# Retention heads with the values projected first, and two of four weight-block sums made by accumulating transfers

## The chip, the core and the metric

The program runs on one core of a Trainium2 chip. TensorE (PE) multiplies, VectorE (DVE) and ScalarE (ACT) do elementwise work and empty PSUM, GpSimd (POOL) does a few small operations, and SyncE (SP) issues the transfers. Each engine works through its own list strictly in order; a semaphore wait in front of an instruction holds up everything behind it on that engine. The metric is the time of one execution on the device, in microseconds; lower is better.

## The reference, cut to what matters

Two layers of a streaming encoder. Each layer projects 528 tokens (16 meta tokens and 512 of the sequence) of width 1024 to 14336 columns, runs a short gated convolution and a retention with four heads on them, gates the two branches and adds them.

```python
for l in range(DEPTH):                                   # DEPTH = 2
    xn = _rmsnorm(h, pre_norm_g[l])
    proj = xn @ w_in[l] + b_in[l]                        # (528, 1024) @ (1024, 14336)
    c_h, c_b, c_c, c_z, r_q, r_k, r_v, r_z, g_a, g_b = jnp.split(proj, split_at, axis=-1)
    y_a = _short_conv_branch(c_h, c_b, c_c, c_z, conv_w[l], conv_b[l], w_conv_out[l])
    y_b = _retention_branch(r_q, r_k, r_v, r_z, ret_gn_g[l], w_ret_out[l])
    y = jax.nn.sigmoid(g_a) * y_a + jax.nn.sigmoid(g_b) * y_b
    h = h + _rmsnorm(y @ w_o[l], post_norm_g[l])

# _retention_branch, one head: dk = 256, dv = 512
q, k = _rope(q, pos), _rope(k, pos) * dk ** -0.5
s = (q @ k.T) * decay_by_distance                        # chunks of 64 tokens
out = s @ v                                              # within a chunk, and over the state
out = (out - mean) * rsqrt(var + GN_EPS) * gn_g * silu(z)
y_b += out @ w_ret_out[rows of this head]
```

## The kernel before

**Products.** Every float32 product is made of three products in PE's float32r format: each operand is split into a high part (a rounded copy, made by ACT, line 142) and a low part (source minus high part, made by DVE, line 143). Activations are kept transposed, feature by token, as two halves of 264 tokens.

**A group.** Most of the input projection is cut into groups of 256 output columns (class `Group`). A group is a two by two block product of Strassen's kind, in Winograd's form, with seven block products instead of eight: `mul` (line 279) issues one of them as 12 matmuls, four slices of the contraction by three float32r passes, so a group is 84 matmuls. On the weight side it needs four sums of blocks: block 0 + block 1 and block 2 + block 1 (line 307, in place, in the upper halves of the staging tiles `raw`), their combination into tile b (line 314), and the fourth, t4 (line 315). Three staging tiles serve a group: a (block 0 and the first sum), b (block 3 and the combination) and c (block 2 and the second sum). SP loads block by block of 256 KB (lines 299, 301, 302). There are six staging tiles, four pairs of split weights (`whi`, `wlo`) and two of the small pair (`whd`, `wld`).

**Order.** The program is a list of jobs written out by hand: groups, output products of a head (`RetOut`, 24 matmuls for each 128 output columns, line 244), output products of the convolution. After each `mul` and after every second contraction slice of an output product `tick()` advances a count, and work put off with `later(delay, fn)` is emitted at the tick it asked for. The last product of a group (`end`) waits in `pending` until the next job has issued its first two; then the group's callback runs: `k_done`, `q_done` (rope, and for q the scores at 8, 10 and 12 ticks), `v_done` (transposing the values, `vtrans`, at 3, 6 and 9 ticks) or `z_done`. `z_done` emits the rest of the head: `attend` (line 481) at 1, 3, 5 and 7 ticks, then the group norm in three steps: `stats` at 10 (line 370, a column sum on PE; line 374 on DVE; line 375, a power, on POOL), `wide` at 13 (line 384, PE spreads the 528 results over the partitions; ACT copies them out, line 387), `finish` at 14 to 17 (DVE scales the four tiles, line 514, and splits them). The next head's output products need all four split tiles. A tile scheduler then fixes the order on each engine; calls in `high_priority` (evictions of PSUM) go ahead of other work.

In the order of a head before, each of heads 1 to 3 projects keys, queries, the first values, then two of the previous head's output products, the second values, the other two, and the two gate groups z. Head 0 of each layer is written out apart and calls the same callbacks.

Of the kernel before, what the change touches and what calls it, by code (L numbers as in the profile page):

```python
# [15 lines left out]
ALU = mybir.AluOpType  # L16
# [40 lines left out]
def trunk(ctx: ExitStack, tc: tile.TileContext, xT, w_in, binT, w_co, w_ro, w_o, gpre, gpost,  # L57
# [19 lines left out]
    def rslot(w=T):  # L77
        return gr.tile([P, w], F32R, tag="r", name=nm("r"))

    def fslot(w=T, dt=F32):  # L80
        return gr.tile([P, w], dt, tag="r", name=nm("f"))
# [45 lines left out]
    def later(delay, fn):  # L127
        now[1] += 1
        heappush(queue, (now[0] + delay, now[1], fn))
# [154 lines left out]
    class Group:  # L284
# [10 lines left out]
        def load(self, j, w):  # L295

            t = self.raw[j] = src()
            if j == 1:
                nc.sync.dma_start(t[:, 512:], w[:, 3, :])
                return  # L300
            nc.sync.dma_start(t[:, 0:512], w[:, j, :])
            nc.sync.dma_start(t[:, 512:], w[:, 1, :])

        def halves(self, j):
            if not j:
                for r in self.raw[0::2]:
                    nc.vector.tensor_tensor(r[:, 512:], r[:, 512:], r[:, 0:512], op=ALU.add)  # L307
            self.w[j] = wtile("whi"), wtile("wlo")
            split(*self.w[j], self.raw[j])

# [79 lines left out]
    def twice(dst, src):  # L390

        nc.scalar.copy(dst.rearrange("p (a b) -> p a b", a=2),
                       src[:, T - CHUNK:T].unsqueeze(1).to_broadcast([P, 2, CHUNK]))
# [402 lines left out]
    for l in range(DEPTH):  # L796
# [20 lines left out]
        def add(job, *args, todo=todo):  # L817
            todo.append((job, args))
            return job

        def k_done(ts, hd):
            a, b, hd["k"] = rope(ts, 0)

            def k8():
                hd["k8"] = rslot(512).rearrange("p (n c) -> p n c", n=4)
                for n in range(4):
                    twice(hd["k8"][:, n, :], hd["k"][n // 2][n % 2].bitcast(F32))
            later(0, a)
            later(2, b)
            later(3, k8)  # L830

        def q_done(ts, hd, h, l, d=8):
            a, b, hd["q"] = rope(ts, QCOLS[l].t0)
            later(0, a)
            later(2, b)

            def tables():
                hd["S"] = [gr.tile([P, SW], F32R, tag="S", name=nm(x), bufs=2) for x in ("Shi", "Slo")]
                nc.sync.dma_start(Dsb, decay[h])
            later(3, tables)  # L840
            for n, js in enumerate(((0,), (1, 2), (3, 4))):
                later(d + 2 * n, lambda js=js: scores(l, hd["q"], hd["k"], hd["k8"], *hd["S"], js))

        def v_done(ts, hd, d=3):
            hd["vt"] = hd.get("vt", []) + list(ts)
            if len(hd["vt"]) == 4:
                vt = hd["vt"]
                v8 = fslot(512).rearrange("p (v c) -> p v c", v=4)
                for v in range(4):
                    twice(v8[:, v, :], vt[v])  # L850
                hd["V"] = V = [(rslot(512), rslot(512)) for _ in JT]
                for n, js in enumerate(((0, 1), (2, 3), (4,))):
                    later(d + 3 * n, lambda js=js: vtrans(vt, v8, V, js))

        def z_done(ts, hd, h, l, yr, silu=(1,)):
            cs = slice(QCOLS[l].t0, T)
            for n in silu:
                nc.scalar.activation(ts[n][:, cs], ts[n][:, cs], AF.Silu)
            hd["zt"] = hd.get("zt", []) + list(ts)
            if len(hd["zt"]) < 4:  # L860
                return

            def start():
                hd["sums"] = fslot()
                hd["n"] = normed(l, hd["zt"], hd["sums"], yr)
            later(0, start)
            for v in range(4):
                later(1 + 2 * v, lambda v=v: attend(l, h, *hd["S"], hd["V"], v, hd["zt"][v], hd["sums"]))
            later(10, lambda: hd["n"][0]())
            later(13, lambda: hd["n"][1]())  # L870
            for v in range(4):
                later(14 + v, lambda v=v: hd["n"][2](v))

        hd["done"] = (k_done, q_done, v_done, z_done)
        yrs = jb["yrs"] = [[] for _ in range(H)]
# [6 lines left out]
        add_conv(0)  # L882
        for h in range(1, H):
            d = {}
            add(Group(l, R_K + h * DK, I_ALL[l], lambda ts, d=d: k_done(ts, d)))
            add(Group(l, R_Q + h * DK, I_Q[l], lambda ts, d=d, h=h, l=l: q_done(ts, d, h, l)))
            add(Group(l, R_V + h * DV, I_ALL[l], lambda ts, d=d: v_done(ts, d)))
            for q in (0, 1):
                add(RetOut(l, h - 1, q), yrs[h - 1])
            add(Group(l, R_V + h * DV + 256, I_ALL[l], lambda ts, d=d: v_done(ts, d)))  # L890
            for q in (2, 3):
                add(RetOut(l, h - 1, q), yrs[h - 1])
            for b in range(2):
                add(Group(l, R_Z + h * DV + b * 256, I_Q[l],
                          lambda ts, d=d, h=h, l=l, yr=yrs[h]: z_done(ts, d, h, l, yr), AF.Silu))
# [364 lines left out]
```

## Time and profile before

| | |
|---|---|
| median of 3 runs | 1603.13 us (1600.23 to 1605.2) |
| profiled execution | 1600.25 us, span of its instructions 1598.4 us |
| PE busy | 1553.9 us, 97% of the span |
| DVE, ACT, POOL busy | 1168.9, 910.2, 28.9 us |
| mean granted TensorE clock | 0.995 |
| transfers | 174.37 MB, mean 109 GB/s |

A matmul's row lasts until its result has left the array, and the next one starts before that; so PE's busy time tells only where it stood still for longer than a matmul's overlap. What a stretch lost is seen from the number of matmuls in it and from the waits of PE. "Idle before" is the time an engine sat still before an instruction, with what released it. PEclk is the granted clock as a share of full speed: 1.00 is 2.4 GHz, 0.5 is 1.2 GHz.

### The profile page before, as it was taken

What the parts mean: (1) busy time and instruction counts of PE and PEld (TensorE: products, weight loads), DVE (VectorE), ACT (ScalarE), POOL (GpSimd) and SP (SyncE); (2) the same over time, 40 slices, a digit from 0 to 9 for tenths busy, and PEclk for the clock granted to TensorE, in tenths of its full rate; (3) what the DMA queues carried; (4) which work ended last, traced back from release to release, by engine and by line L of the source; (5) the groups of instructions that cost most, each with busy time, mean ns of one, the idle gap of its engine ahead of it and who ended that gap; (6) DMA issues with size and microseconds to landing.
All of it is one profiled execution on the core that took longest, in us unless ns stands there. A gap on an engine that the chain in (4) does not pass through costs nothing.

```text
span 1598.4 us, 29227 instructions
## 1 busy us (share of the span) xinstructions
PE 1553.9 (97%) x11762; PEld 1494.1 (93%) x11762; DVE 1168.9 (73%) x1702; ACT 910.2 (57%) x1763; POOL 28.9 (2%) x23
## 2 busy tenths in 40 slices
PE   9999999899999999999999999999999999999998
PEld 9989999898999999999999998998998999999986
DVE  6996966776776788866376889678777777997542
ACT  6675565464565466655345666655654655676531
POOL 0000000001000000000000000000000000000000
PEclk9999999999999999999999999999999999999999
DMA  7132332232222243335321223222322223334421
GB/s 263 67 113 73 106 107 89 83 108 97 89 103 87 91 141 128 133 123 180 119 101 53 100 94 113 103 103 95 111 93 80 101 98 119 132 126 145 142 98 53
DMA packets 86039, 174.37 MB, mean 109 GB/s; under 512 B 11280, under 2 KB 15888, under 8 KB 85904
## 3 DMA queue, kind: packets, MB, share of 16 engines
q1 hardware_dynamic: 85760, 172.50, 31.2%
q8 instruction: 92, 1.51, 0.4%
q14 instruction: 43, 0.35, 0.1%
q10 hardware_dynamic: 144, 0.01, 0.0%
HBM read 168.21 MB, written 4.26 MB: 108 GB/s over the span
## 4 chain that ended last, share of the span: by engine, by line
PE 79%; DVE 10%; ACT 5%; issue 3%; DMA 3%; POOL 1%; SPq 0%; DVEq 0%; POOLq 0%; ACTq 0%
PE pb L279 25%; PE pp L244 15%; PE pc L279 13%; PE pp L648 7%; PE pa L279 6%; PE pp L481 4%; PE pp L1122 3%; PE pb L648 3%; DVE wlo L143 2%; PE pp L422 2%; DMA raw<-in_w_in 2%; ACT whi L142 2%; DVE r L143 1%; PE pp L384 1%; PE pp L447 1%
## 5 line engine op out<-in xcount | busy, mean ns | idle before, releaser
L143 DVE TENSOR_TENSOR wlo<-raw,whi 128x1024 fp32r<-128x1024 f32 (+2 forms) x358 | 392.7, 1107 | 120.4 <-ACT whi L142 117.5
L142 ACT CAST whi<-raw 128x1024 fp32r<-128x1024 f32 (+2 forms) x358 | 339.4, 959 | 227.8 <-PE pp L244 63.7
L279 PE MATMUL pb<-Xh,whi 128*128 128x264 f32 (+2 forms) x1008 | 287.7, 285 | 2.2 <-ACT pa L335 1.2
L279 PE MATMUL pb<-Xl,whi 128*128 128x264 f32 (+2 forms) x1008 | 285.0, 283 | 0.0
L279 PE MATMUL pb<-Xh,wlo 128*128 128x264 f32 (+2 forms) x1008 | 284.7, 283 | 0.1
L244 PE MATMUL pp<-r,whi 128*128 128x264 f32 (+1 forms) x1152 | 251.2, 325 | 5.6 <-ACT r L142 4.8
L279 PE MATMUL pc<-Xh,whi 128*128 128x264 f32 (+2 forms) x672 | 194.4, 289 | 8.1 <-ACT f L325 7.8
L244 PEld LDWEIGHTS pp<-r,whi 128*128 128x128 f32 x1152 | 176.3, 188 | 23.7 <-ACT r L142 5.9
L279 PEld LDWEIGHTS pb<-Xh,whi 128*128 128x128 f32 x1008 | 189.6, 188 | 4.4 <-ACT pa L335 1.6
L279 PE MATMUL pc<-Xl,whi 128*128 128x264 f32 (+2 forms) x672 | 192.0, 286 | 0.0
L279 PE MATMUL pc<-Xh,wlo 128*128 128x264 f32 (+2 forms) x672 | 191.5, 285 | 0.0
L279 PEld LDWEIGHTS pb<-Xl,whi 128*128 128x128 f32 x1008 | 189.6, 188 | 0.6
L279 PEld LDWEIGHTS pb<-Xh,wlo 128*128 128x128 f32 x1008 | 189.3, 188 | 0.5 <-DVE wlo L143 0.3
L244 PE MATMUL pp<-r,wlo 128*128 128x264 f32 (+1 forms) x576 | 153.1, 321 | 1.4 <-DVE wlo L143 1.4
L307 DVE TENSOR_TENSOR raw<-raw 128x512 f32<-128x512 f32 x168 | 115.1, 686 | 41.4 <-DMA raw<-in_w_in 40.9
L279 PEld LDWEIGHTS pc<-Xh,whi 128*128 128x128 f32 x672 | 128.0, 190 | 12.3 <-ACT f L325 11.2
L279 PEld LDWEIGHTS pc<-Xl,whi 128*128 128x128 f32 x672 | 127.9, 190 | 0.4
L279 PEld LDWEIGHTS pc<-Xh,wlo 128*128 128x128 f32 x672 | 127.8, 190 | 0.3
L244 PEld LDWEIGHTS pp<-r,wlo 128*128 128x128 f32 x576 | 95.3, 188 | 9.8 <-DVE wlo L143 2.0
L279 PE MATMUL pb<-Xh,whd 128*128 128x264 f32 (+2 forms) x336 | 96.7, 288 | 1.1 <-ACT f L325 1.1
L279 PE MATMUL pa<-Xh,whi 128*128 128x264 f32 (+2 forms) x336 | 96.7, 288 | 0.0
L279 PE MATMUL pa<-Xl,whi 128*128 128x264 f32 (+2 forms) x336 | 95.7, 285 | 0.0
(219 smaller groups left out, 3300.3 us busy)
## 6 DMA issues: line engine op xcount, KB each, us to landing
raw<-in_w_in SPq DMA_DIRECT2D x426, 256.0 KB, 2.9
raw<-in_w_ro SPq DMA_DIRECT2D x32, 512.0 KB, 3.2
raw<-in_w_in SPq DMA_DIRECT2D x20, 512.0 KB, 4.8
raw<-in_w_co SPq DMA_DIRECT2D x16, 512.0 KB, 3.2
raw<-in_w_o SPq DMA_DIRECT2D x16, 512.0 KB, 3.9
Dsb<-in_decay SPq DMA_DIRECT2D x8, 520.0 KB, 3.9
h1d<-f SPq DMA_DIRECT2D x8, 264.0 KB, 4.5
f<-h1d SPq DMA_DIRECT2D x8, 264.0 KB, 4.3
```

Source lines behind the costliest of these rows:

```text
L142: nc.scalar.copy(dst_hi, src)
L143: nc.vector.tensor_tensor(dst_lo, src, dst_hi.bitcast(F32), op=ALU.subtract)
L244: nc.tensor.matmul(banks[i][:, 0:cols.n], wt(k)[:, msl], xs(k)[:, sl], start=(k == 0 and a == 0), stop=(k == nk - 1 and a == 2),)
L279: nc.tensor.matmul(o[:, 0:n], wt[:, k, :], xs[:, blk, k, HALF - n:], start=(first and k == 0 and a == 0), stop=(k == 3 and a == 2), skip_g ...
L307: nc.vector.tensor_tensor(r[:, 512:], r[:, 512:], r[:, 0:512], op=ALU.add)
L384: nc.tensor.matmul(pp[:, c // per, (c % per) * sc:(c % per + 1) * sc], y[:, c:c + 1].to_broadcast([sc, P]), ident[0:sc, 0:sc], start=True, ...
L422: nc.tensor.matmul(pp[0:kn, n + i, 0:cols.n], k[dt][x][:, k0:k0 + kn] if j < 4 else k8[:, dt * 2 + x, :], q[dt][y][:, sl], start=(dt == 0 ...
L447: nc.tensor.transpose(pp[0:kn, b, v * P:(v + 1) * P], vt[v][:, k0:k0 + kn] if j < 4 else v8[:, v, :], ident)
L481: nc.tensor.matmul(pp[:, b, lo_ - banks[b][0]:hi_ - banks[b][0]], V[j][x][0:kn, v * P:(v + 1) * P], S[0:kn, SOFF[j] + lo_ - q0:SOFF[j] + h ...
L648: nc.tensor.matmul(o, wt(k), xs[:, i0:], start=(k == 0 and a == 0), stop=(k == KD - 1 and a == 2))
L1122: nc.tensor.matmul(o, x[:, xs], wo[k][half][w], start=(k == 0 and a == 0), stop=(k == KD - 1 and a == 2))
```

## The change

Three things change. (1) Loading: tiles a and c are filled by one transfer that writes block j into both halves (a broadcast source, 512 KB), and a second transfer, issued by POOL, adds block 1 to the upper half while it is written. The two DVE additions of line 307 go. (2) A head now projects its values first, then the keys, then two output products of the head before, then the queries, the other two output products, and the gates. (3) The values are transposed at 34, 37 and 40 ticks after the second value group, which falls into the gate groups; the small copies for it come at 32, and the tiles for the result are taken at 34. `wide` comes at 14 ticks in place of 13, `finish` at 15 to 18.

```diff
@@ -298,13 +298,10 @@
             if j == 1:
                 nc.sync.dma_start(t[:, 512:], w[:, 3, :])
                 return
-            nc.sync.dma_start(t[:, 0:512], w[:, j, :])
-            nc.sync.dma_start(t[:, 512:], w[:, 1, :])
+            nc.sync.dma_start(t.rearrange("p (a c) -> p a c", a=2), w[:, j:j + 1, :].to_broadcast([P, 2, 512]))
+            nc.gpsimd.dma_start(t[:, 512:], w[:, 1, :], accum_op=ALU.add)
 
         def halves(self, j):
-            if not j:
-                for r in self.raw[0::2]:
-                    nc.vector.tensor_tensor(r[:, 512:], r[:, 512:], r[:, 0:512], op=ALU.add)
             self.w[j] = wtile("whi"), wtile("wlo")
             split(*self.w[j], self.raw[j])
 
@@ -845,12 +842,20 @@
             hd["vt"] = hd.get("vt", []) + list(ts)
             if len(hd["vt"]) == 4:
                 vt = hd["vt"]
-                v8 = fslot(512).rearrange("p (v c) -> p v c", v=4)
-                for v in range(4):
-                    twice(v8[:, v, :], vt[v])
-                hd["V"] = V = [(rslot(512), rslot(512)) for _ in JT]
+                hd["V"] = V = []
+
+                def places():
+                    V.extend((rslot(512), rslot(512)) for _ in JT)
+
+                def v8():
+                    hd["v8"] = fslot(512).rearrange("p (v c) -> p v c", v=4)
+                    for v in range(4):
+                        twice(hd["v8"][:, v, :], vt[v])
+
+                later(d - 2, v8)
+                later(d, places)
                 for n, js in enumerate(((0, 1), (2, 3), (4,))):
-                    later(d + 3 * n, lambda js=js: vtrans(vt, v8, V, js))
+                    later(d + 3 * n, lambda js=js: vtrans(vt, hd["v8"], V, js))
 
         def z_done(ts, hd, h, l, yr, silu=(1,)):
             cs = slice(QCOLS[l].t0, T)
@@ -867,9 +872,9 @@
             for v in range(4):
                 later(1 + 2 * v, lambda v=v: attend(l, h, *hd["S"], hd["V"], v, hd["zt"][v], hd["sums"]))
             later(10, lambda: hd["n"][0]())
-            later(13, lambda: hd["n"][1]())
+            later(14, lambda: hd["n"][1]())
             for v in range(4):
-                later(14 + v, lambda v=v: hd["n"][2](v))
+                later(15 + v, lambda v=v: hd["n"][2](v))
 
         hd["done"] = (k_done, q_done, v_done, z_done)
         yrs = jb["yrs"] = [[] for _ in range(H)]
@@ -882,12 +887,12 @@
         add_conv(0)
         for h in range(1, H):
             d = {}
+            for n in range(2):
+                add(Group(l, R_V + h * DV + n * 256, I_ALL[l], lambda ts, d=d: v_done(ts, d, 34)))
             add(Group(l, R_K + h * DK, I_ALL[l], lambda ts, d=d: k_done(ts, d)))
-            add(Group(l, R_Q + h * DK, I_Q[l], lambda ts, d=d, h=h, l=l: q_done(ts, d, h, l)))
-            add(Group(l, R_V + h * DV, I_ALL[l], lambda ts, d=d: v_done(ts, d)))
             for q in (0, 1):
                 add(RetOut(l, h - 1, q), yrs[h - 1])
-            add(Group(l, R_V + h * DV + 256, I_ALL[l], lambda ts, d=d: v_done(ts, d)))
+            add(Group(l, R_Q + h * DK, I_Q[l], lambda ts, d=d, h=h, l=l: q_done(ts, d, h, l)))
             for q in (2, 3):
                 add(RetOut(l, h - 1, q), yrs[h - 1])
             for b in range(2):
```

On PE, in layer 0, where head 2's first group follows head 1's gates: the stretch from the column sum (`pp<-ones_d`) to the spread (`pp<-ident,ny`), with the first matmul of each block product in it. Before:

```order
L370 MATMUL pp_3435<-ones_d,f_3148 88x1 x6
L279 MATMUL pb_3262<-Xh,whi_3188 128x264
...
L279 MATMUL pb_3475<-Xh,whi_3254 128x264
...
L384 MATMUL pp_3503<-ident,ny_3443 128x88 x6
L279 MATMUL pc_3476<-Xh,whi_3254 128x264
```

After:

```order
L367 MATMUL pp_3391<-ones_d,f_3124 88x1 x6
L279 MATMUL pb_3236<-Xh,whi_3164 128x264
...
L279 MATMUL pb_3426<-Xh,whi_3228 128x264
...
L279 MATMUL pc_3427<-Xh,whi_3228 128x264
...
L279 MATMUL pb_3236<-Xh,whd_3171 128x264
...
L381 MATMUL pp_3474<-ident,ny_3399 128x88 x6
L279 MATMUL pb_3426<-Xh,whi_3294 128x264
```

Two block products (24 matmuls) stood between the two; now there are four (48), the closing product of the last gate group among them.

On DVE, in the same place, the end of `finish` (`f<-f,f` of line 514 or 511 scales a tile, `r<-f,r` of line 143 is its low part, lines 403 to 405 are rope). Before:

```order
L143 TENSOR_TENSOR wlo_3513<-raw_3120,whi_3512 128x1024
L143 TENSOR_TENSOR r_3533<-f_2830,r_3532 128x528
L403 TENSOR_TENSOR f_3549<-f_3259,cos_sb 128x528
L404 TENSOR_TENSOR f_3550<-f_3260,sin_sb 128x528
L514 TENSOR_TENSOR f_2954<-f_2954,f_3502 128x528
L405 TENSOR_TENSOR f_3549<-f_3549,f_3550 128x528
L143 TENSOR_TENSOR wlo_3594<-raw_3192,whi_3593 128x1024
L143 TENSOR_TENSOR r_3555<-f_3549,r_3554 128x528
L143 TENSOR_TENSOR wld_3734<-t_3631,whd_3733 128x512
L143 TENSOR_TENSOR r_3560<-f_2831,r_3559 128x528
L143 TENSOR_TENSOR wlo_3635<-raw_3324,whi_3634 128x1024
L143 TENSOR_TENSOR r_3578<-f_2953,r_3577 128x528
```

After:

```order
L511 TENSOR_TENSOR f_2719<-f_2719,f_3473 128x528
L511 TENSOR_TENSOR f_2720<-f_2720,f_3473 128x528
L511 TENSOR_TENSOR f_2904<-f_2904,f_3473 128x528
L143 TENSOR_TENSOR r_3497<-f_2719,r_3496 128x528
L511 TENSOR_TENSOR f_2905<-f_2905,f_3473 128x528
L143 TENSOR_TENSOR r_3515<-f_2720,r_3514 128x528
L143 TENSOR_TENSOR wlo_3520<-raw_3168,whi_3519 128x1024
L143 TENSOR_TENSOR r_3537<-f_2904,r_3536 128x528
L143 TENSOR_TENSOR r_3555<-f_2905,r_3554 128x528
L353 TENSOR_TENSOR f_3424<-f_3424,f_3425 128x528
L143 TENSOR_TENSOR wlo_3563<-raw_3298,whi_3562 128x1024
```

The rope of keys and queries is gone from between them: from the statistics (`nv`) to the low part of the fourth tile stood 31 DVE instructions, and now stand 13.

On POOL, in the same place, where there was nothing but the powers. After:

```order
L302 DMA raw_3168<-in_w_in 128x512
L302 DMA raw_3300<-in_w_in 128x512
L372 TENSOR_TENSOR ny_3399<-nv_3398,mhalf 88x6
L302 DMA raw_3458<-in_w_in 128x512
L302 DMA raw_3568<-in_w_in 128x512
```

Each power (13 of them in norms) now has accumulating transfers ahead of it in POOL's list, 168 in all, and each of these waits for the load of its tile.

## Rows read from the trace of the kernel before

**Rows 1.** The page: span, busy time of each engine, its share, instructions.
```profile
span 1598.4 us, 29227 instructions
PE 1553.9 (97%) x11762; PEld 1494.1 (93%) x11762; DVE 1168.9 (73%) x1702; ACT 910.2 (57%) x1763; POOL 28.9 (2%) x23
```

**Rows 2.** Stretches: length, busy time (instructions) of five engines, PEclk, DMA share, GB/s.
```profile
560.00:600.00 40.00, 40.00 (x332) 40.00 (x331) 32.99 (x45) 27.16 (x47) 0.00 (x0) 1.00 0.39 137
270.00:310.00 40.00, 35.36 (x274) 34.38 (x273) 32.36 (x48) 19.18 (x37) 4.71 (x1) 0.96 0.21 74
385.00:420.00 35.00, 30.15 (x233) 29.23 (x232) 29.06 (x44) 17.16 (x35) 4.71 (x1) 0.95 0.20 70
1070.00:1100.00 30.00, 26.62 (x195) 24.67 (x194) 27.43 (x41) 16.17 (x34) 2.65 (x1) 1.00 0.24 83
```

**Rows 3.** Waits of PE: total, times, longest, from 270 to 310 us.
```profile
PE pp L384 <- POOL ny L375: 3.0, 1, 3.0
PE pp L244 <- ACT r L142: 1.1, 1, 1.1
PE pp L370 <- DVE f L496: 0.4, 1, 0.4
```

**Rows 4.** The columns of rows 2, stretches in which the granted clock fell.
```profile
284.60:288.10 3.50, 3.50 (x18) 3.50 (x18) 1.95 (x3) 1.98 (x6) 0.00 (x0) 0.51 0.00 0
397.20:400.70 3.50, 3.50 (x19) 3.50 (x18) 1.80 (x3) 1.64 (x6) 0.00 (x0) 0.52 0.06 25
141.20:148.20 7.00, 6.86 (x35) 6.89 (x36) 4.24 (x6) 2.52 (x6) 1.71 (x1) 0.51 0.11 37
```

**Rows 5.** The wait of PE from 124 to 150 us.
```profile
PE pp L370 <- DVE f L496: 3.3, 1, 3.3
```

**Rows 6.** Waits of PE from 1070 to 1100 us.
```profile
PE pc L279 <- ACT f L325: 1.6, 1, 1.6
PE pp L244 <- ACT r L142: 1.3, 1, 1.3
```

**Rows 7.** PE in order of time: start, length, and the idle time before.
```profile
275.98 1.07 PE L370 MATMUL pp<-ones_d,f 128*88 128x1 f32 x12 [0.35 <-DVE f L496]
283.11 1.57 PE L384 MATMUL pp<-ident,ny 88*128 88x88 f32 x12 [3.01 <-POOL ny L375]
```

**Rows 8.** The powers on POOL in order of time: start, length.
```profile
278.34 4.71 POOL L375 TENSOR_TENSOR ny<-nv,mhalf 88x6 f32<-88x6 f32 x1 [132.93 <-DVE nv L374]
504.63 1.32 POOL L375 TENSOR_TENSOR ny<-nv,mhalf 88x6 f32<-88x6 f32 x1 [108.03 <-DVE nv L374]
```

**Rows 9.** DVE there, in order of time.
```profile
129.95 0.69 DVE L314 TENSOR_TENSOR raw<-raw,raw 128x512 f32<-128x512 f32 x1 [2.50 <-DMA raw<-in_w_in]
131.01 0.69 DVE L307 TENSOR_TENSOR raw<-raw 128x512 f32<-128x512 f32 x1 [0.36 <-DMA raw<-in_w_in]
138.49 0.69 DVE L307 TENSOR_TENSOR raw<-raw 128x512 f32<-128x512 f32 x1 [1.60 <-DMA raw<-in_w_in]
```

**Rows 10.** Transfers: count, KB each, median us from issue to landing.
```profile
raw<-in_w_in SPq DMA_DIRECT2D x426, 256.0 KB, 2.9
raw<-in_w_ro SPq DMA_DIRECT2D x32, 512.0 KB, 3.2
sin_sb<-in_sinT SPq DMA_DIRECT2D x1, 264.0 KB, 7.0
```

**Rows 11.** A wait of PE over the whole span.
```profile
PE pc L279 <- ACT f L325: 7.8, 9, 1.6
```

**Rows 12.** Waits of PE from 104 to 113 us, where head 0's values are transposed.
```profile
PE pc L279 <- ACT f L325: 2.1, 2, 1.2
```

**Rows 13.** DVE by line: busy, mean ns, idle before, releaser.
```profile
L307 DVE TENSOR_TENSOR raw<-raw 128x512 f32<-128x512 f32 x168 | 115.1, 686 | 41.4 <-DMA raw<-in_w_in 40.9
L314 DVE TENSOR_TENSOR raw<-raw,raw 128x512 f32<-128x512 f32 x84 | 57.7, 687 | 39.1 <-DMA raw<-in_w_in 39.0
```

**Rows 14.** SP's issues of two blocks for consecutive tiles, in order of time.
```profile
127.47 0.33 SPq L301 DMA_DIRECT2D raw<-in_w_in  x1
134.88 0.33 SPq L301 DMA_DIRECT2D raw<-in_w_in  x1
```

## The prediction

> **What bounds the kernel now.** I read the page's busy times first: PE is busy 97% of the span, DVE 73%, ACT 57% [rows 1]. The change leaves PE's matmuls as they are, in number and shape, so only time in which PE stands still, or runs at a lower clock, can be won. Then the stretches. In a stretch of groups alone, from 560 to 600 us, PE is busy 40.00 of 40 us and does 332 matmuls [rows 2]; that is 0.1205 us each and 84 x 0.1205 = 10.1 us for a group, which is full pace. Where one head follows another it is not: 35.36 us of 40 with DVE busy 32.36, 30.15 of 35 with DVE 29.06, and in layer 1 26.62 of 30 with DVE 27.43 [rows 2]. There DVE is the fullest engine. The waits of PE say what ends last: the power on POOL 3.0 us, a split tile of the head's result 1.1 us, the column sum's operand 0.4 us [rows 3].
>
> Behind the 3.0 us wait the granted clock is 0.51 for 3.5 us, the lower of the two levels (1.2 GHz); the same follows the same wait in the second transition, and the wait of 3.3 us in head 0's end is followed by 7.0 us at 0.51 [rows 4, 5]. Layer 1's waits of 1.6 and 1.3 us [rows 6] are not followed by one: its stretch stands at 1.00 [rows 2].
>
> **Term 1, the transitions of layer 0 (heads 1 to 2 and 2 to 3).** Each loses its idle time, 40 - 35.36 = 4.64 and 35 - 30.15 = 4.85 us [rows 2], and half of 3.5 us at the lower clock, 1.75 us each [rows 4]: 13.0 us together. Now the causes. From the column sum to the spread, 275.98 to 283.11, pass 7.13 us [rows 7]. PE has the column sum itself (1.07 us) and 24 matmuls (2.9 us) to do in it, and the 3.0 us wait is most of what is left. In the new order 48 matmuls stand there, 5.8 us; with 1.07 that makes 6.9 of the 7.13 us, so the wait shrinks to 0.3 us even if the power takes as long as now. It need not: the same power takes 4.71 us in this transition, with DVE crowded, and 1.32 us at 504 us, where no rope follows [rows 8]. With a wait that short I expect no drop of the clock, as in layer 1. The wait for the split tile goes because DVE has 13 instructions from the statistics to the fourth tile's low part instead of 31; the rope now stands behind it. I take 0.7 us to remain in each: a gain of 11.6 us, between 5 (one cause stays in each) and 13.0.
>
> **Term 2, the same in layer 1.** Two transitions of 30 - 26.62 = 3.38 us [rows 2], 6.8 us in all, with the waits in [rows 6]. The first is ACT waiting in order behind the spread, which waits for the power; the second is the split tile again. I take 5.8 us, between 2 and 6.8.
>
> **Term 3, head 0 of layer 0.** The column sum waits 3.3 us for DVE and the clock is low for 7.0 us, so 3.3 + 3.5 = 6.8 us [rows 4, 5]. DVE comes late there because it stands at the head of its list waiting for loads: 2.50 us for line 314, 0.36 and 1.60 us for line 307 [rows 9]. Line 307 goes, with 2 x 0.69 us of work: 3.3 us in this stretch. The wait of line 314 stays, since it needs tile c's load, now 512 KB (3.2 us to landing where w_ro's were measured, against 2.9 for 256 KB [rows 10]). That is just enough to end PE's wait, or not quite. I take half, 3.4 us, between 0 and 6.8. Over the whole span line 279 waits 7.8 us for ACT's evictions [rows 11]; 2 x 1.6 of it is in term 2 and 2.1 in term 5's row [rows 12]. Of the 2.5 us left, DVE's and ACT's shorter lists may save 1 us.
>
> **Term 4, the additions themselves.** 168 x 0.686 = 115.1 us and 40.9 us of waiting leave DVE [rows 13]. In stretches where PE already runs at full pace DVE was busy 32.99 of 40 us [rows 2], so there it is worth nothing; where DVE was full, terms 1 to 3 have counted it.
>
> **Term 5, what moves into other stretches.** The rope of the keys now runs beside the first output products, that of the queries beside the last two. There DVE also empties PSUM for the output products; the nearest row is the wait for a split tile, 1.1 us [rows 3], six times (heads 1 to 3, both layers): 0 to 6.6 us, and I take 1, since line 307 is gone there too. The values are transposed beside the gate groups, where ACT has the silu and its splits as well, with ten evictions of 512 columns more. The row for a transposing stretch in which ACT and DVE are loaded is head 0's: PE lost 2.1 us to ACT's evictions [rows 12]. Six times that is 12.6, 0 is the other bound; I take 5.
>
> **Term 6, the accumulating transfers.** The trace has none. An upper half used to be ready after its load and a DVE addition; now a wait on POOL, an issue by POOL and a second landing come between. What hides it is the ring of six tiles: two blocks are loaded 7.4 us apart (127.47 to 134.88 [rows 14]), and line 314 does not read tile a before tile c's load, a later one, has landed; tile c's own sum is needed only by ACT's split after that. So the transfer has about 7 us. Bounds for issue and landing: 2.9 us, as a plain load of that size, and 14 us, twice the slowest of [rows 10], since it reads the old contents too. I take 6 us, twice a load, nearer to the many rows than to the one: cost 0. If the cover is gone, DVE waits in order at line 311, once a group.
>
> The Trainium skill (DMA: Bandwidth & Descriptors, Anatomy of one DMA, SWDGE path) puts a transfer issued by GpSimd at 2.0 us plus its bytes over 436 GB/s; for 256 KB that gives 2.6 us as an estimate, and by it the term is 0 as well. No run here shows one so far.
>
> **Sum.** 11.6 + 5.8 + 3.4 + 1 = 21.8 us gained, 1 + 5 = 6 lost: 15.8. The profiled execution took 1600.25 us, 1598.4 of it the span; that gives 1584.5. The median of the runs, 1603.13, lies 2.9 us higher, so I predict 1587.
>
> **Rivals.**
> (a) The gain is eaten in the gate groups. ACT gets ten evictions more in a pair of gate groups, and PE's next product needs banks that ACT empties. For it: the 2.1 us of [rows 12], which came with less on ACT. Against: ACT is busy only 27.16 of 40 us in groups alone [rows 2]. At 3.5 us in each of six stretches 21 us go and 1603 stays.
> (b) DVE's relief is worth more than I count: all of 13.0, 6.8 and 6.8 us and nothing lost elsewhere, 26.6 us, and some 5 us of smaller waits: 1603 - 32 = 1571.
> (c) Slower: POOL's list becomes what paces the groups. Two accumulating transfers a group of 10.1 us leave 5.05 us for each, if POOL is held while it issues. From there on each tenth counts twice a group. At 5.5 us, over the some 40 groups that stand without output products between them (of a layer 14 of the convolution and 6 of the closing gates), it is 40 x 0.9 = 36 us: 1603 - 16 + 36 = 1623. The powers behind them would come late as well. For it: the one thing POOL does now is stretched from 1.32 to 4.71 us beside a full DVE [rows 8]. Against: nothing in the trace says that an issue takes that long; SP's take 0.33 us [rows 14].
> By the Trainium skill (SBUF — State Buffer, Who interferes with whom) a DVE instruction with two SBUF operands contends with a GpSimd instruction that reads SBUF, not with one that only writes. The two powers of [rows 8] agree; by it an issue that only writes descriptors would not be stretched, which speaks against (c).
> (d) Slower: the accumulating transfer lands later than its 7 us. DVE's idle time in a group is 10.1 x (1 - 32.99/40) = 1.8 us and the removed additions give 1.4 more, so it decides from about 10 us. At 10.5 us, 84 x 0.5 = 42 us: 1629.
>
> **How the numbers follow.** Forecast (a gain of 8 to 25 us) 0.56; (a) 0.14, of it 0.08 no change, 0.04 faster and 0.02 slower; (b) 0.10; (c) 0.12, of it 0.02 no change; (d) 0.08, of it 0.02 no change. No change is within 0.3%, 4.8 us, about what a measurement of this kernel can tell. So faster 0.56 + 0.04 + 0.10 = 0.70, same 0.12, slower 0.02 + 0.10 + 0.06 = 0.18. The range goes from (b), 1571, to 1612, which takes in (a) and the beginning of (c) and (d); it leaves out most of (c), (d) and a little of (b). The likeliest case alone would be 1578 to 1595.
>
> **What would show it.** Term 1: the spread's wait for POOL under 0.5 us, and PEclk 1.00 in the transitions of layer 0. Term 2: no wait of line 279 for ACT before the spread. Term 3: the column sum of head 0 waits under 1.5 us. Term 5: waits of PE for ACT in the gate groups, about 1 us a head. Term 6: line 311 waits for the load of tile c by SP, not for POOL's transfer. The forecast is wrong if POOL's rows fill the groups, if DVE or ACT wait for transfers issued by POOL, or if PE waits in the gate groups as long as it did between the heads.

## The result, and the profile after

The changed kernel takes 1586.7 us (median, 1586.35 to 1589.07) against 1603.67 beside it: a ratio of 0.99, interval 0.9881 to 0.9919, so 17 us faster. The profiled execution's span is 1584.4 us, 14.0 less than before. From here on "the old order" is that of before, "the new order" that of the change; the line numbers of the changed kernel are three lower (line 311 is 314 of before, 322 is 325, 367 is 370, 372 is 375, 381 is 384, 493 is 496), and line 302 is the accumulating transfer.

The page after: busy time of the engines, then the accumulating transfer's group on POOL (busy, mean ns, idle before), then the transfers (count, KB, median us from issue to landing).

```profile
span 1584.4 us, 29320 instructions
PE 1545.0 (98%) x11762; PEld 1490.3 (94%) x11762; DVE 1073.9 (68%) x1534; ACT 910.1 (57%) x1763; POOL 166.1 (10%) x191
...
L302 POOL DMA_DIRECT2D raw<-in_w_in x168 | 146.9, 875 | 1105.9 <-DMA raw<-in_w_in 543.7
...
raw<-in_w_in SPq DMA_DIRECT2D x188, 512.0 KB, 3.9
raw<-in_w_in POOLq DMA_DIRECT2D x168, 256.0 KB, 3.7
raw<-in_w_in SPq DMA_DIRECT2D x90, 256.0 KB, 3.4
```

DVE lost 95 us of work [rows 1] and POOL gained 137, with 168 issues of 0.875 us. More bytes come in than before (218.42 MB against 174.37, the difference being the accumulating transfers), in longer pieces, and they land later: 3.9 us for a 512 KB load and 3.7 for an accumulating transfer, where 256 KB took 2.9 [rows 10].

The stretches that answer to those of [rows 2], and after them three of the six gate-group stretches into which the values' transposing has moved, and one of a low clock (columns as in [rows 2]):

```profile
266.00:306.00 40.00, 39.61 (x328) 39.35 (x327) 30.24 (x42) 21.42 (x40) 4.88 (x5) 1.00 0.41 119
375.00:410.00 35.00, 34.89 (x289) 34.62 (x289) 26.88 (x39) 18.43 (x35) 4.02 (x4) 1.00 0.41 121
1050.00:1080.00 30.00, 30.00 (x225) 28.97 (x224) 20.97 (x30) 17.39 (x36) 2.82 (x3) 1.00 0.43 124
```

```profile
236.00:250.00 14.00, 12.82 (x102) 12.28 (x101) 9.99 (x13) 11.95 (x26) 1.73 (x2) 1.00 0.48 135
344.00:358.00 14.00, 12.57 (x100) 12.02 (x99) 9.99 (x13) 12.03 (x27) 1.75 (x2) 1.00 0.51 139
1028.00:1042.00 14.00, 12.94 (x100) 12.40 (x100) 10.07 (x13) 11.30 (x25) 1.74 (x2) 1.00 0.54 153
1413.00:1416.50 3.50, 3.50 (x19) 3.50 (x19) 3.17 (x4) 2.62 (x5) 0.88 (x1) 0.56 0.45 147
```

The reader is to see two things. The transitions are at full pace: 39.61 of 40 us where it was 35.36, 34.89 of 35, 30.00 of 30, PEclk 1.00 in all three, and DVE is busy 30.24, 26.88 and 20.97 us where it was 32.36, 29.06 and 27.43. And the gate groups are not: PE is busy 12.6 to 12.9 of 14 us, ACT 11.3 to 12.0.

Waits of PE over the whole span (total, times, longest), and the powers of the two transitions on POOL, 4.71 us each before ([rows 8] has the first; the second ran from 391.89):

```profile
PE pc L279 <- ACT f L322: 15.0, 13, 2.6
PE pp L367 <- DVE f L493: 1.2, 2, 0.8
```

```profile
274.94 1.35 POOL L372 TENSOR_TENSOR ny<-nv,mhalf 88x6 f32<-88x6 f32 x1 [2.90 <-DVE nv L371]
382.84 1.35 POOL L372 TENSOR_TENSOR ny<-nv,mhalf 88x6 f32<-88x6 f32 x1 [2.98 <-DVE nv L371]
```

DVE during the first of them stands still; its next instruction after the statistics, in order of time:

```profile
277.15 1.23 DVE L143 TENSOR_TENSOR wlo<-raw,whi 128x1024 fp32r<-128x1024 f32 x1 [2.29 <-ACT whi L142]
```

No wait of line 381 for POOL is left (6.5 us in four waits before). But line 279's wait for ACT's evictions has grown from 7.8 us [rows 11] to 15.0. Of it, 3.8 us lie in the transposing stretches of layer 1, and 7.0 us, the largest part, where the prediction expected nothing: in the closing gate groups at the end of each layer (0.9 us before). This is how its longest, 2.6 us, comes about; in order of time, SP and then DVE, ACT, PE:

```profile
622.64 0.37 SPq L301 DMA_DIRECT2D raw<-in_w_in  x1
```

```profile
627.82 0.69 DVE L311 TENSOR_TENSOR raw<-raw,raw 128x512 f32<-128x512 f32 x1 [3.45 <-DMA raw<-in_w_in]
628.43 0.70 DVE L571 TENSOR_TENSOR f<-f,f 128x528 f32<-128x528 f32 x1
```

```profile
631.52 1.17 ACT L142 CAST r<-f 128x528 fp32r<-128x528 f32 x2 [3.75 <-DVE f L571]
633.65 1.28 ACT L322 ACT_TABLE_LOAD   x1
```

```profile
635.76 0.39 PE L279 MATMUL pc<-Xh,whi 128*128 128x264 f32 x1 [2.59 <-ACT f L322]
```

Tile c's 512 KB load is issued at 622.64. Line 311 needs its lower half, and stands at the head of DVE's list for 3.45 us until 627.82, 5.2 us after the issue. The convolution branch's product (line 571) is queued behind it; ACT's casts `r<-f` wait 3.75 us in order for those products; the evictions of line 322 stand behind the casts and a table load of 1.28 us; and PE waits for the bank that they empty. The other two long waits (1.2 us at 592 and 2.3 at 1411) follow the same list: line 311 starts 6.2 us after the issue of tile c's load there (579.32 to 585.47) and 5.6 us (1397.86 to 1403.45).

### The profile page after: what moved, and what is told of

It reads as the page before. It is cut to its first block, busy times and chain, and to the rows that moved or that the text cites. A ratio compares the mean times of both kernels' runs of the same rounds, so it can differ in the third digit from the quotient of the medians.

```text
span 1584.4 us, 29320 instructions
## 1 busy us (share of the span) xinstructions
PE 1545.0 (98%) x11762; PEld 1490.3 (94%) x11762; DVE 1073.9 (68%) x1534; ACT 910.1 (57%) x1763; POOL 166.1 (10%) x191
## 2 busy tenths in 40 slices
DMA packets 107544, 218.42 MB, mean 138 GB/s; under 512 B 11280, under 2 KB 15888, under 8 KB 107408
## 4 chain that ended last, share of the span: by engine, by line
PE 74%; DVE 9%; ACT 8%; DMA 5%; issue 4%; DVEq 0%; POOLq 0%; ACTq 0%
PE pb L279 22%; PE pp L244 16%; PE pc L279 11%; PE pp L645 8%; PE pa L279 5%; DMA raw<-in_w_in 5%; PE pp L478 4%; DVE wlo L143 3%; PE pb L645 3%; PE pp L1127 3%; ACT whi L142 2%; PE pp L419 1%; ACT f L322 1%; ACT r L452 1%; ACT r L451 1%
## 5 line engine op out<-in xcount | busy, mean ns | idle before, releaser
L302 POOL DMA_DIRECT2D raw<-in_w_in x168 | 146.9, 875 | 1105.9 <-DMA raw<-in_w_in 543.7
L244 PE MATMUL pp<-r,whi 128*128 128x264 f32 (+1 forms) x1152 | 245.6, 321 | 0.0
L311 DVE TENSOR_TENSOR raw<-raw,raw 128x512 f32<-128x512 f32 x84 | 57.9, 690 | 93.1 <-DMA raw<-in_w_in 78.2
```

What stands on the lines that cost most here:

```text
L244: nc.tensor.matmul(banks[i][:, 0:cols.n], wt(k)[:, msl], xs(k)[:, sl], start=(k == 0 and a == 0), stop=(k == nk - 1 and a == 2),)
L302: nc.gpsimd.dma_start(t[:, 512:], w[:, 1, :], accum_op=ALU.add)
L311: nc.vector.tensor_tensor(b[:, 0:512], a[:, 512:], c[:, 0:512], op=ALU.add)
```

## The experiments

Each ratio is to the kernel before, run on the same chip in the same rounds. The waits of line 279's `pc` products for ACT's evictions in the closing groups of the two layers tell most of them apart, so they stand here once for all (us, read from the waits of PE from 560 to 680 us and from 1340 to 1480; each from one profiled execution):

| kernel | ratio (interval) | layer 0 | layer 1 |
|---|---|---|---|
| before | 1 | 0.4 | 0.5 |
| new order alone | 0.9901 (0.9885 to 0.9917) | 0 | 0 |
| accumulation alone | 1.0046 (1.0031 to 1.0062) | 4.7 | 4.7 |
| the change | 0.99 (0.9881 to 0.9919) | 3.8 | 3.2 |
| the change again, on another chip | 0.9897 (0.9876 to 0.9918) | 3.3 | 2.3 |
| the change, tile a alone accumulated | 0.9873 (0.9852 to 0.9894) | 2.6 | 1.8 |
| the change, block loaded in two halves | 0.986 (0.9841 to 0.9879) | 1.2 | 0.6 |
| block in two halves again, on another chip | 0.9847 (0.9832 to 0.9862) | 0 | 2.5 |
| accumulation alone, two halves | 0.9956 (0.9941 to 0.9972) | 0 | 1.3 |
| two halves, closing gates plain | 0.9846 (0.9827 to 0.9866) | 0.3 | 0 |

**The new order without the accumulating transfers.** Loads and line 307 as before, everything else as changed:

```diff
-            nc.sync.dma_start(t.rearrange("p (a c) -> p a c", a=2), w[:, j:j + 1, :].to_broadcast([P, 2, 512]))
-            nc.gpsimd.dma_start(t[:, 512:], w[:, 1, :], accum_op=ALU.add)
+            nc.sync.dma_start(t[:, 0:512], w[:, j, :])
+            nc.sync.dma_start(t[:, 512:], w[:, 1, :])
...
```

> The new order of a head with the loads of the kernel before (two plain transfers into tiles a and c, two additions on DVE). Theory O, that the order alone takes the waits out of the transitions between heads (terms 1 and 2, 19 us of stalls and low clock in the trace of before): 1588 to 1593 us, PE waits for the power under 0.5 us, no low clock in the transitions, but the wait of head 0's column sum stays near 3 us (term 3). Rival A, that DVE's relief by the accumulating transfers is what emptied the transitions: 1596 us or more, and DVE still over 80% busy there.

1591.84 us (1585.77 to 1592.46), ratio 0.9901. Waits of PE over the span, head 0's column sum and the stretch behind it (columns as in [rows 2]), and the power of the first transition:

```profile
PE pc L279 <- ACT f L325: 12.1, 13, 1.6
PE pp L370 <- DVE f L496: 4.6, 3, 3.3
```

```profile
141.32 1.89 PE L370 MATMUL pp<-ones_d,f 128*88 128x1 f32 x12 [3.31 <-DVE f L496]
```

```profile
141.00:148.00 7.00, 6.68 (x34) 6.71 (x35) 4.24 (x7) 2.71 (x6) 1.71 (x1) 0.51 0.11 37
```

```profile
281.15 1.32 POOL L375 TENSOR_TENSOR ny<-nv,mhalf 88x6 f32<-88x6 f32 x1 [135.76 <-DVE nv L374]
```

And the closing group of the chain above: tile c's lower half on SP, line 314 on DVE:

```profile
619.49 0.33 SPq L301 DMA_DIRECT2D raw<-in_w_in  x1
```

```profile
622.53 0.69 DVE L314 TENSOR_TENSOR raw<-raw,raw 128x512 f32<-128x512 f32 x1
```

The order alone gives the whole gain, with DVE as loaded as before (1169.6 us busy). The power takes 1.32 us and nothing waits for it. Head 0's wait of 3.31 us stays, with the low clock behind it (0.51), so its removal (term 3) is the accumulation's doing. In the closing groups PE waits for nothing: line 314 runs 3.0 us after its load's issue. So all of line 279's 12.1 us lie outside of the closing groups, where the change has 15.0 less 7.0, that is 8.0: the accumulating transfers save some 4 us there, and the closing groups take back 7.0.

**The accumulating transfers without the new order.** The diff of the loading alone, in the kernel before.

> The order of the kernel before with the accumulating transfers. Theory O: term 3 is won (head 0's column sum waits under 1.5 us, no low clock there, 6 us), the transitions keep the rope and half of their stalls, and the groups alone lose 5 to 8 us to DVE standing at line 311 for tile c's load: 1596 to 1602 us. Rival A: 1592 us or less.

1614.14 us (1610.94 to 1617.94), ratio 1.0046: slower. Waits of PE, the power of the first transition, and the mean granted clock:

```profile
PE pc L279 <- ACT f L322: 15.7, 14, 2.9
PE pp L381 <- POOL ny L372: 3.6, 3, 3.1
```

```profile
274.73 4.74 POOL L372 TENSOR_TENSOR ny<-nv,mhalf 88x6 f32<-88x6 f32 x1 [4.48 <-DVE nv L371]
```

```profile
core 0: 1613.4 us, clock 0.989
```

The first transition keeps a power of 4.74 us and a wait for it of 3.1. Head 0's column sum waits 0.6 us and no low clock follows it, but the closing groups wait 9.4 us, and the clock is 0.989 against 0.995, which over the span is (0.995 - 0.989) x 1613 = 10 us of full pace: there are eight stretches of 3.4 or 6.8 us at the lower level where before had three (the end of the program left out in both). The accumulation as written costs more than it gives.

**The spread at 13 ticks again.** The changed kernel with `wide` at 13 and `finish` at 14 to 17 (the diff shows the first); the scheduler then puts 36 matmuls, not 48, between column sum and spread.

```diff
-            later(14, lambda: hd["n"][1]())
+            later(13, lambda: hd["n"][1]())
```

> The changed kernel with the spread at 13 ticks and the finish at 14 to 17, as before: 36 matmuls between column sum and spread in place of 48. If the longer way to the spread is what removed the wait (distance, as the prediction's term 1 had it: 7.13 us needed, 36 x 0.1205 + 1.07 = 5.4 us there), PE waits 1.7 us for the power in each transition of layer 0, and the time is 3 to 5 us over the changed kernel's: 1590 to 1592. If it is the shorter power beside an emptier DVE (1.35 us in the changed kernel against 4.71), the spread does not wait and the time is the same within 1.5 us.

1593.34 us (1592.31 to 1595.99), ratio 0.9916 (0.9901 to 0.9931), not to be told from the change. The column sum and the spread on PE, and the power between them:

```profile
273.15 0.21 PE L367 MATMUL pp<-ones_d,f 128*88 128x1 f32 x1
...
278.54 0.24 PE L381 MATMUL pp<-ident,ny 88*128 88x88 f32 x1
```

```profile
274.58 1.35 POOL L372 TENSOR_TENSOR ny<-nv,mhalf 88x6 f32<-88x6 f32 x1 [2.90 <-DVE nv L371]
```

The power ends at 275.93, 2.6 us before the spread, and nothing waits. Even with 24 matmuls (2.9 us) and the 1.07 us of the column sum, the spread would have stood at 277.1. The distance is not what took the wait away; the shorter power is. (That 24 would do is worked out from these rows, not run.)

**The block loaded in two halves.** The changed kernel, with two loads of 256 KB, the lower half first, in place of one of 512 KB:

```diff
-            nc.sync.dma_start(t.rearrange("p (a c) -> p a c", a=2), w[:, j:j + 1, :].to_broadcast([P, 2, 512]))
+            nc.sync.dma_start(t[:, 0:512], w[:, j, :])
+            nc.sync.dma_start(t[:, 512:], w[:, j, :])
             nc.gpsimd.dma_start(t[:, 512:], w[:, 1, :], accum_op=ALU.add)
```

> The changed kernel with block j loaded into the two halves by two plain transfers of 256 KB, the lower half first, in place of one broadcast transfer of 512 KB. Line 311 reads the lower half of c alone. If the stalls in the closing groups (1.2 and 2.6 us at 590 and 633 us, 2.3 at 1409 us with 1.7 us of low clock) come from the longer landing of the 512 KB load (3.9 us median against 2.9), they shrink and the time falls by 2 to 5 us: 1582 to 1585. If they come from the traffic or from the order of DVE's list, the time stays within 1.5 us of 1586.7 or rises by the second issue on SP.

1582.44 us (1581.42 to 1589.45), ratio 0.986. The issue of tile c's lower half and line 312 (311 of the change), at the place of the chain above:

```profile
621.66 0.33 SPq L301 DMA_DIRECT2D raw<-in_w_in  x1
```

```profile
625.88 0.69 DVE L312 TENSOR_TENSOR raw<-raw,raw 128x512 f32<-128x512 f32 x1 [2.02 <-DMA raw<-in_w_in]
```

Line 312 now runs 4.2 us after the issue and has stood for 2.02 us, not 3.45; 5.2 us were between them in the change and 3.0 in the order alone. Repeated on another chip beside the change itself:

> The kernel of e6_c_split_load beside after_control on one chip. Theory 1: 3 to 6 us under after_control, ratio to before 0.984 to 0.988. Rival: level with it within 2 us.

> The changed kernel as it is, beside e10_gates_plain and e6_again on one chip. Theory 1: the 512 KB load costs it about 4 us against two loads of 256 KB, ratio to before 0.988 to 0.992. Rival: the two are level, and the difference between them seen so far was the chip's.

1583.65 us, ratio 0.9847 (0.9832 to 0.9862), and 1590.88 us, ratio 0.9897 (0.9876 to 0.9918): the two intervals are apart, so the one load of 512 KB costs the change about 0.4 to 0.5%, 7 us, against two of 256 KB.

**The same in the old order.**

> The order of before, accumulating transfers, and block j loaded by two transfers of 256 KB. Theory 1: what made the accumulation alone slower by 7 us was the landing time of the 512 KB load in the closing groups and the low clock behind its waits; then this is level with before or a little faster (head 0's wait is gone), ratio 0.995 to 1.001. Rival: the accumulating transfer itself (a second write of each upper half, POOL's list) costs it; then the ratio stays at 1.003 to 1.006.

1600.49 us (1596.35 to 1608.49), ratio 0.9956. Its waits, and the power of the first transition:

```profile
PE pc L279 <- ACT f L323: 8.1, 10, 1.6
PE pp L382 <- POOL ny L373: 1.9, 4, 0.7
```

```profile
275.14 2.98 POOL L373 TENSOR_TENSOR ny<-nv,mhalf 88x6 f32<-88x6 f32 x1 [3.97 <-DVE nv L372]
```

Theory 1 holds: 0.9% between this and the accumulation alone is the load's form. And the parts add up: 0.9901 and 0.9956 together make 0.9857; the kernel with both has 0.986. The power takes 2.98 us here and 4.74 in the accumulation alone, both with the rope beside it and without the additions. What tells them apart is where DVE first pauses. Two neighbouring instructions of DVE, first in the kernel before, where this power runs from 278.34 to 283.05, then here, where it runs from 275.14 to 278.12:

```profile
281.17 0.70 DVE L405 TENSOR_TENSOR f<-f,f 128x528 f32<-128x528 f32 x1
282.57 0.71 DVE L143 TENSOR_TENSOR r<-f,r 128x528 fp32r<-128x528 f32 x1 [0.70 <-ACT r L142]
```

```profile
276.21 0.70 DVE L402 TENSOR_TENSOR f<-f,cos_sb 128x528 f32<-128x528 f32 x1
277.03 1.23 DVE L143 TENSOR_TENSOR wlo<-raw,whi 128x1024 fp32r<-128x1024 f32 x1
```

Before, DVE ran without a pause until 281.87, and the power ended 1.2 us later; here DVE pauses for 0.1 us at 276.91, and the power again ends 1.2 us later. The same holds, within 1.18 to 1.23 us, for every power of 88 x 6 values that started beside a busy DVE in before, the change, the order alone, the accumulation alone and here. So the rope stretches the power by keeping DVE busy without a pause, and one short pause is enough for POOL. PE's wait for the power is 1.9 us in all here, 6.5 before.

**Tile a alone accumulated.** Tile c by two plain loads and line 307's addition.

> The changed kernel, but only tile a is filled by the long load and the accumulating transfer; tile c by two plain loads and a DVE addition, as before. Theory 1: the stalls of the closing groups come from tile c's 512 KB load, for which line 311 stands in order on DVE; without it they fall from 1 to 3 us to under 1 us, and with DVE relieved of half the additions head 0's column sum waits between 0.8 and 3.6 us: 1580 to 1586 us. Rival: they come from the greater traffic of all transfers together; then halving the accumulating ones leaves half of the stalls: 1586 to 1591 us.

1588.42 us (1585.27 to 1591.17), ratio 0.9873. Tile c's second load on SP and its addition (line 311 here) on DVE:

```profile
622.65 0.42 SPq L303 DMA_DIRECT2D raw<-in_w_in  x1
```

```profile
627.25 0.69 DVE L311 TENSOR_TENSOR raw<-raw 128x512 f32<-128x512 f32 x1 [3.26 <-DMA raw<-in_w_in]
```

Theory 1 of this run fails, and the rival is nearer: without tile c's long load the closing groups still wait 2.6 and 1.8 us, 4.4 of the change's 7.0. A plain 256 KB load, beside tile a's long load and its accumulating transfer, needs 4.6 us here (622.65 to 627.25), and DVE stands for it 3.26 us, nearly as long as in the change. So it is not the 512 KB of tile c by itself; the loads around it make each other late. The form of the load counts too, since cutting it in two keeps the bytes and takes the waits from 7.0 us to 1.8 (5.6 to 2.5 in the repetition). In the two-halves kernel the lower half lands 3.2 us after its issue (median), the upper half 3.7 after its own, the whole block in the change 3.8: line 311 gains by waiting for the lower half alone. Whether the broadcast source costs anything by itself, and how much the added bytes count, the runs do not tell.

**The values transposed early.** The changed kernel with `v_done` called with 3 ticks, not 34, in heads 1 to 3.

> The changed kernel, but the values of heads 1 to 3 are transposed right after the second value group (ticks 3, 6, 9) instead of in the gate groups (34, 37, 40). Theory 1: the transposing is cheap wherever it stands, and only its meeting with the silu and splits of the gate groups costs 1.0 to 1.4 us in each of six stretches; taken out of them, that idle time goes there and the new place, where ACT is busy 21.4 of 40 us, loses little: 1579 to 1584 us. Rival: the new place is the one where the head before is being finished, so its split tiles or the evictions come late again, 1 to 4 us a head, some of them with a low clock behind them: 1588 to 1600 us.

1669.24 us (1667.35 to 1671.21), ratio 1.0376 (1.0356 to 1.0397): the rival's direction and far past its size. The scores (line 419) on PE by line, first here, then in the change:

```profile
L419 PE MATMUL pp<-r,r 128*128 128x448 f32 (+5 forms) x264 | 56.7, 373 | 28.0 <-DVE r L143 15.6 <-ACT r L142 11.7
```

```profile
L419 PE MATMUL pp<-r,r 128*128 128x448 f32 (+5 forms) x264 | 43.0, 308 | 0.0
```

The scores wait 28.0 us and the output products (line 244) 21.2, where neither waited; the clock falls to 0.983. The scores of a head now come in one piece (36 matmuls in a row in layer 0, where the change has mostly 12), and the low part of the rope that they need stands on DVE behind a sum that waits for a load:

```profile
1063.89 0.69 DVE L311 TENSOR_TENSOR raw<-raw,raw 128x512 f32<-128x512 f32 x1 [3.36 <-DMA raw<-in_w_in]
1064.50 0.68 DVE L143 TENSOR_TENSOR r<-f,r 128x512 fp32r<-128x512 f32 x1
```

So this moved more than the transposing, and doesn't price term 5; it says only that this order of projections, as it is scheduled here, needs the late transposing.

**One pass of the transposing's evictions on DVE.** The two-halves kernel, with this in `vtrans`:

```diff
-                nc.scalar.activation(hi[0:kn], pv, AF.Identity, bias=s)
+                nc.vector.tensor_scalar(hi[0:kn], pv, s, None, op0=ALU.add)
```

> Like e6_c_split_load (two loads of 256 KB instead of one of 512 KB), and in the transposing of the values the second of the two ACT passes over each PSUM tile (adding the mean, 128 x 512) is made by DVE. Theory 1: the transposing stretches wait for ACT, busy 12 of 14 us there, while DVE has 2 to 4 us to spare; six stretches lose about 0.8 to 1.2 us less and head 0's stretch too: 3 to 7 us under e6_c_split_load, 1576 to 1580. Rival: what PE waits for there is the chain product, first pass with its sum, second pass, free bank, whichever engine does the second pass: within 2 us of e6_c_split_load.

1588.26 us (1583.33 to 1591.47), ratio 0.9866 (0.9844 to 0.9887), level with the two-halves kernel, as the rival said. Its wait for the second part of a transposed tile:

```profile
PE pp L479 <- DVE r L458: 6.8, 8, 1.7
```

It was 1.7 us in two in the two-halves kernel: what ACT was spared, PE now waits for DVE.

**Plain loads in the closing gates.** The two-halves kernel; only groups below column `G_A` accumulate.

> Like e6_c_split_load (two loads of 256 KB and an accumulating transfer) in all groups but the closing gates of each layer, which load plainly and add on DVE as before. Theory 1: accumulation pays in head 0 of layer 0 (the column sum's wait and the low clock behind it) and costs in the closing groups, where its landing lengthens the time from a staging tile's release to its next use; taken out there, the stalls of 1.3 us near 632 and 0.8 us near 1408 go: 1 to 3 us under e6_c_split_load. Rival: the stalls are the product, the cast of the output and the table load in order on ACT, and stay as they are: within 1 us of it.

1580.94 us (1578.67 to 1587.49), ratio 0.9846, the lowest median, but level with the two-halves kernel beside it (0.9847). Its waits and clock:

```profile
PE pc L279 <- ACT f L328: 6.6, 10, 1.2
```

```profile
core 0: 1576.9 us, clock 0.999
```

The waits of the closing groups go, from 1.2 and 0.6 (0 and 2.5 in its repetition) to 0.3 and 0, as theory 1 said; what that is worth, 1 to 3 us, these runs cannot tell from nothing.

## Why the prediction was right

The time, 1587 against 1586.7, is nearer than its steps were. Terms 1 to 3 gave 4.5 us more than forecast (25.3 against 20.8), and term 6 cost 7.6 where nothing was forecast; that the errors nearly cancel is luck. What the prediction had right is the place of the gain: the waits between the heads and in head 0, and the low clock behind them.

- **Term 1** (11.6 us): about 12.5 of the 13.0 us came, by the stretches. But its reason was wrong. The prediction put the spread farther behind the column sum and took the power at its old length, with a wait of 0.3 us left. The power fell from 4.71 to 1.35 us because no rope runs beside it (DVE stands still for 2.29 us there); with 36 matmuls nothing waits either. The prediction named a shorter power as possible and didn't use it. Its reading that DVE is the fullest engine there holds for layer 1 alone (27.43 us against 26.62 of PE); in layer 0 PE was busier.
- **Term 2** (5.8 us): all 6.8; no wait of PE from 1050 to 1085 us or in the second transition, from 1150 to 1190.
- **Term 3** (3.4 us, half): mis-sized. The column sum waits 0.8 us, not 3.3, and no low clock follows: about 6 of 6.8 us. With the additions kept, wait and low clock stay, and with the accumulation alone they go; so the cause was rightly placed at line 307. The 1 us added for other evictions did not come: line 279 waits longer, not less.
- **Term 5** (-5, and -1 for the rope): 14 us less the busy time of each of the six stretches (12.82, 12.57, 12.56, 12.94, 12.93, 12.93) makes 7.3 us, a little more than 5 and well under rival (a)'s 21. In its old places, 14 us each in before, the transposing had cost 0.5 us in all. The profiled execution is a mild one: in the repetition of the change the clock also falls for 3.4 us behind two of these stretches (0.58 from 354.3 to 357.8 us). For the rope nothing is found.
- **Term 6** (0): this is the step that failed. "So the transfer has about 7 us" of cover, and the cost 0: the closing groups wait 7.0 us, 6.1 more than before, and behind the one at 1409 us the clock stands at 0.56 for 3.5 us. The transfer itself was inside its bounds (0.875 us of issue and 3.7 to landing, against 6 taken), and as predicted line 311 waits mostly for tile c's load by SP, 72.1 us in 43 waits. For POOL's transfer it waits in four, by the view of line 302's waiters:

```profile
  DVE raw L311: 9.0, 4
```

(One of the four, at 1403 us, ended with SP's load, which landed 1.3 us after POOL's transfer.) What was missed is that the plain load in front of it grew to 512 KB, and that in the closing groups line 311 stands in order for it until 5.2 to 6.2 us after its issue. The prediction had the number for 512 KB (3.2 us) and used it in term 3 alone; and it took the cover from a stretch of head 0, not from the closing groups, where ACT and DVE wait on each other in order.

By these, 12.5 + 6.8 + 6 - 7.3 - 6.1 - 1.5 (the low clock) = 10.4 us, of 14.0 between the two profiled spans. Of the 3.6 us left, 1.4 are two waits of output products for split weights (line 244 for `wlo`), which are gone; the rest I have not followed one by one.

Of the prediction's signs of being wrong, two came in part: DVE waits for POOL's transfers, if only in a few places, and PE loses 7.3 + 7.0 us in the gate groups, not far from the 16.3 us between the heads before (9.5 in layer 0, 6.8 in layer 1).

The rivals: (b) needed no loss anywhere, and 1571 was not reached even by the best kernel here. (c) is out: POOL is busy 10%, an issue takes 0.875 us and not 5.05. (d) has the right place and the wrong transfer: DVE did wait in order at line 311 and it did cost, for SP's load most of all, and in the closing groups. In the old order that was enough for the slower side.

On the pages that the prediction named: the accumulating transfer lands 3.7 us after issue. By the Trainium skill (DMA: Bandwidth & Descriptors, Anatomy of one DMA, SWDGE path), 2.0 us plus the bytes over 436 GB/s, the estimate for a transfer by GpSimd of that size was 2.6; the measurement decides. By the Trainium skill (SBUF — State Buffer, Who interferes with whom) a DVE instruction with two SBUF inputs contends with a GpSimd instruction that reads SBUF, and not with one that only writes it. The trace agrees: the issues, taken as only writing, took 862 ns at least, 872 in the middle and 1053 at most over 168, while the power, which reads SBUF, took from 1.35 to 4.74 us.

## What to carry to other kernels

Read what an engine's ordered list does beside a slow instruction before moving work away in time: here the short power, not the longer distance, took the wait away, and a new order of the jobs was worth more than 95 us of removed DVE work. When an addition is handed to the DMA, look at the load in front of it: here a consumer waited for it in order, and loading the piece that is read first by itself helped. And test the two halves of a change apart: one gave all of the gain, the other was worth 0.4% more once its load was cut in two.

## What the runs showed of the hardware

A transfer of 256 KB that adds while it writes lands 3.7 us after POOL's issue (4.2 in the two-halves kernel), and holds POOL for 0.87 us. Loads are slower beside such transfers: 256 KB by SP takes 2.9 us (median) before, 3.1 with tile a alone accumulated and 3.5 in the two-halves kernel. The power of 88 x 6 values on POOL takes 1.32 to 1.35 us while DVE stands still, and 2.98 to 4.74 while DVE runs rope and low parts; it then ends 1.2 us after the first pause of DVE, however short (0.1 us in the two-halves kernel of the old order).
